# One lasting pool of weight tiles, and slabs in the space of an early part, in a one-core decoder layer

## The chip, the cores and the metric

The kernel runs on one core of a Trainium2 chip. Times are device microseconds (us). Three runs of the kernel before gave 1140.43, 1143.43 and 1144.64 us; the metric is the median, 1143.43 us.

## The reference

One decoder layer on x of 512 tokens by 2048 columns, in float32. h = RMSNorm(x); one combined projection of h (2048 columns to q, three pairs of k and v, gates, and four inputs of a second mixer); an attention mixer of 16 query heads in 4 groups with three branches (compressed, selected and window keys); a gated recurrence (HGRN2) of 8 heads; per-head RMSNorm and SiLU gates; one output projection, the residual, and a last RMSNorm. The piece that matters here is the compressed branch, which needs k and v in overlapping blocks of 32 tokens:

```python
def rmsnorm(x, g):
    xf = x.astype(jnp.float32)
    y = xf * lax.rsqrt(jnp.mean(xf * xf, axis=-1, keepdims=True) + EPS)
    return (y * g.astype(jnp.float32)).astype(x.dtype)

def compress_blocks(kv, pe, w1, w2):
    B, S, G, dh = kv.shape
    n_cmp = (S - CMP_BLOCK) // CMP_STRIDE + 1
    idx = CMP_STRIDE * np.arange(n_cmp)[:, None] + np.arange(CMP_BLOCK)[None, :]
    blk = kv[:, idx] + pe[:, None, :]
    blk = blk.transpose(0, 1, 3, 2, 4).reshape(B, n_cmp, G, CMP_BLOCK * dh)
    return jax.nn.gelu(blk @ w1) @ w2
...
    kc = compress_blocks(k_cmp, pe_k, w1_k, w2_k)
    vc = compress_blocks(v_cmp, pe_v, w1_v, w2_v)
    logits = jnp.einsum('btgrd,bngd->bgrtn', q, kc).astype(jnp.float32) - slopes * dist_c
...
    o = g[..., 0:1] * o_cmp + g[..., 1:2] * o_slc + g[..., 2:3] * o_win
```

## The kernel before

All large products are in float32 with each operand split in two parts of a shorter type: `hi` is a cast (ScalarE, L301) and `lo` the rest (VectorE, L302), and every product is three matmuls, hi x hi, hi x lo and lo x hi. A weight tile `w` is 128 partitions x 1024 float32, 4 KB a partition; a loaded tile takes one tile for the raw weights and two for its parts. Loads of weights are issued on SP's queue (`load_raw`, L160; in the seven-product part also L416). h^T lies in SBUF in 16 blocks of 128x512, each as hi and lo (`hh_`, `hl_`).

The program has two parts. In the first, k and v of the compressed branch (`first_proj`, `second_proj`) and two value projections are made, sums of blocks of h^T are formed (`all_sums`; the spaces `s2` and `s14`), and two wide projections are computed with seven block products in place of eight (`seven`, L405 to L505; products L453 to L455, plain ones L463 to L465; `in_turn` keeps two loads ahead). For these, `third_sums` saves block 21 of h^T to DRAM by POOL (L390) and puts a sum in its place; `block_21_back` brings it back, by POOL (L398). The results `y` are finished by `z_done` and stored to DRAM by POOL (L539). `first_part` holds the spaces of this part: `s2`, `s14`, twenty weight tiles `w`, and `e`.

When the first part is closed, a second pool of ten weight tiles (WBUF) and one of 25 slabs (`sl()`, 128x512 float32 each) take its space, so that their first tiles wait for the last use of what lay there. Then:

- `blocks(kf, 32)` loads k in two shifted copies by POOL (L607 to L610) into slabs, and VectorE adds the position terms (L621); `masks` and some clearing follow on POOL.
- `make_kd(0, 0)` and `make_q(0)` are projections (`proj_fm`: matmuls L555 to L557, 24 of them to a weight tile), run in turn with `compress` of k (weights L628, matmuls L637, a GELU, then L653). What they make is split and copied between partition halves on SP's queue (`split_dma`, L682 to L687); POOL casts the copies into the window's keys (L707, L708).
- `rows_back(vt_scr)` loads the value tokens `v_tok` into four slabs on SP's queue (L1072); `blocks(vf, 48)` does for v what was done for k.
- `make_kd(0, 1)`, `make_q(1)` and `make_kd(1, 0)` run in turn with `compress` of v. Attention, the recurrence, gates and the output projection follow, with the other projections as filling.

A scheduler sets the order on each engine from the program's priorities and its own times of the operations; each engine then works through its order. DMA issues wait in their queue's order, and a queue's DMAs go round on eight semaphores (`DMAHW0` to `DMAHW7` for SP, `DMASW0` to `DMASW7` for POOL).

Of the kernel before, what the change touches and what calls it, by code (L numbers as in the profile page):

```python
# [17 lines left out]
P = 128  # L18
# [11 lines left out]
WCOLS = 1024  # L30
WBUF = 10
NSLAB = 25
# [1 line left out]
PJ = 4  # L34
AHEAD = 2
FILL = (44, 42, 40, 24)
NU = 20
NE = 8
PAIRS = 6
AHEAD7 = 2  # L40
# [3 lines left out]
C_Q, C_KC, C_VC, C_KS, C_VS, C_KW, C_VW, C_GT, C_ZA = 0, 1024, 1280, 1536, 1792, 2048, 2304, 2560, 2608  # L44
C_QH, C_FH, C_IH, C_ZH = 3632, 4656, 5680, 6704
# [3 lines left out]
def hymba_layer(ctx: ExitStack, tc: tile.TileContext, x, norm_in, w_in, pe_k, w1_k, w2_k,  # L49
                pe_v, w1_v, w2_v, lower_bounds, nsa_norm, hgrn_norm, w_out, final_norm, out):  # L50
    nc = tc.nc
# [7 lines left out]
    small = ctx.enter_context(tc.tile_pool(name="small", bufs=2))  # L59
    psum = ctx.enter_context(tc.tile_pool(name="psum", bufs=1, space=bass.MemoryType.PSUM))  # L60

    cnt = [0, 0]

    def nm(s):
        cnt[0] += 1
        return f"{s}_{cnt[0]}"


    space, first_part = {}, ExitStack()
    wbufs = [NU]  # L70
    for name in ("s2", "s14", "w", "e"):
        space[name] = first_part.enter_context(tc.tile_pool(name=name + "_first", bufs=1))
    scr = ctx.enter_context(tc.tile_pool(name="scr", bufs=1, space=bass.MemoryType.DRAM))

    def sl(dt=FP32):
# [2 lines left out]
    def ev():  # L78
        return space["e"].tile([P, 512], FP32, name=nm("e"), tag="e", bufs=NE)

    def dram(shape=(P, 512)):
        n = nm("d")
        return scr.tile(list(shape), FP32, name=n, tag=n, bufs=1)
# [5 lines left out]
        return big.tile([P, 2048], dt, name=nm(tag), tag=tag, bufs=1)  # L89

    def b4(dt):
        return space["w"].tile([P, WCOLS], dt, name=nm("w"), tag="w", bufs=wbufs[0])

    def pj():
        return psum.tile([P, 512], FP32, name=nm("pj"), tag="pj", bufs=PJ)
# [13 lines left out]
    def run(*gens):  # L109

        st = [[g, t, 0.0] for g, t in gens]
        while st:
            e = min(st, key=lambda e: e[2] / e[1])
            try:
                c = next(e[0])
                e[2] = max([o[2] / o[1] for o in st if o is not e]) * e[1] + 1e-6 if c is None else e[2] + c
            except StopIteration:
                st.remove(e)

    def chain(*gens):  # L120
        for g in gens:
            yield from g
# [35 lines left out]
    def load_raw(src, k0, kt, c0, c):  # L158
        raw = b4(FP32)[:, 0:kt * c].rearrange("p (k c) -> p k c", k=kt)
        nc.sync.dma_start(out=raw, in_=src[k0 * P:(k0 + kt) * P, c0:c0 + c].rearrange("(k p) c -> p k c", p=P))  # L160
        return raw
# [4 lines left out]
    for k0, kt in FIRST:  # L166
        cs = slice(k0 * P, (k0 + kt) * P)
        first_w.append(load_raw(w_in2, k0, kt, C_KC, 256))
        if kt == 2:
            w = b4(FP32).rearrange("p (t c) -> p t c", t=4)  # L170
            for i in range(2):
                nc.sync.dma_start(out=w[:, 2 * i:2 * i + 2],
                                  in_=x2[i * 256:(i + 1) * 256, cs].rearrange("(t p) c -> p t c", p=P))
            xt.append([w[:, t] for t in range(NT)])
        else:
            w = [b4(FP32).rearrange("p (t c) -> p t c", t=2) for _ in range(2)]
# [177 lines left out]
    def corner(q, part):  # L354
        return hb[part][q][:, 0:4:2, 256:512]
# [30 lines left out]
    def third_sums():  # L386

        for q in range(PAIRS // 2):
            for part in range(2):
                nc.gpsimd.dma_start(out=a21[part][q], in_=corner(q, part).bitcast(FP32))  # L390
            hi, lo = [corner(q, part) for part in range(2)]
            nc.scalar.copy(hi, s3[q])
            nc.vector.tensor_tensor(lo, s3[q], hi.bitcast(FP32), ALU.subtract)

    def block_21_back():
        for q in range(PAIRS // 2):
            for part in range(2):
                nc.gpsimd.dma_start(out=corner(q, part).bitcast(FP32), in_=a21[part][q])  # L398
# [1 line left out]
    w_half = w_in2.rearrange("(j h p) c -> h p j c", h=2, p=P)  # L400
    free_banks = [(pj, pj), (pj, pj), (ps_lp, ps_lp), (ps_tp, ps_ot)]

    def seven(c0, done):


        t2, banks, acc, room = {}, {}, {}, {}
# [33 lines left out]
        def give(*names):  # L440
            for name in names:
                free_banks.append(banks[name])
# [24 lines left out]
        def after_first():  # L467
            room["u2"], room["u3"] = [ev(), ev()], [ev(), ev()]
            for tt in range(2):
                nc.scalar.copy(room["u2"][tt], acc["1"][tt])  # L470
            for tt in range(2):
                add(room["u2"][tt], acc["6"][tt], room["u2"][tt])
                add(room["u3"][tt], acc["7"][tt], room["u2"][tt])
            give("6", "7")

        def after_second():
            for tt in range(2):
                done(0, tt, acc["1"][tt], ev())
            for tt in range(2):
                y = ev()  # L480
                add(y, acc["4"][tt], room["u3"][tt])
                done(0, 2 + tt, y, y)
            give("4", "1")
# [34 lines left out]
    def in_turn(steps):  # L518
        ready = []
        for n in range(len(steps) + AHEAD7):  # L520
            if n < len(steps):
                ready.append(steps[n][0]())
            if n >= AHEAD7:
                steps[n - AHEAD7][1](ready[n - AHEAD7])
# [3 lines left out]
    vt_scr = [dram() for _ in range(NT)]  # L528
# [5 lines left out]
    def z_done(which):  # L534
        def done(half, t, src, y):
            th = ev()
            nc.scalar.activation(th, src, AF.Tanh, scale=rs[:, 1, t:t + 1])
            nc.vector.scalar_tensor_tensor(y, th, 1.0, src, ALU.add, ALU.mult)
            nc.gpsimd.dma_start(out=z_scr[which][half][t], in_=y)  # L539
        return done  # L540
# [49 lines left out]
    vc_bd, v_tok = [], []  # L590
# [10 lines left out]
    def blocks(acc, pcol):  # L601

        kv = []
        for j in range(2):
            f = acc[j]
            e, o = sl(), sl()
            nc.gpsimd.dma_start(out=e[0:64, :], in_=f[0:64, :])  # L607
            nc.gpsimd.dma_start(out=e[64:128, 0:511], in_=f[0:64, 1:512])
            nc.gpsimd.dma_start(out=o[0:64, :], in_=f[64:128, :])
            nc.gpsimd.dma_start(out=o[64:128, 0:511], in_=f[64:128, 1:512])  # L610
            kv += [e, o]
        blk = [sl() for _ in range(4)]
        for uq in range(4):
            b4_ = blk[uq].rearrange("p (u g n) -> p u g n", u=4, g=4)
            nc.gpsimd.memset(b4_[:, :, :, 31:32], 0.0)
            pe = col[:, pcol + uq * 4:pcol + uq * 4 + 4].unsqueeze(2).broadcast_to([P, 4, 31])
            for g in range(4):
                src = kv[g].rearrange("p (n u two) -> p u n two", u=8, two=2)
                n0 = uq // 2
                sv = src[:, (uq % 2) * 4:(uq % 2) * 4 + 4, n0:n0 + 31, 0]  # L620
                nc.vector.tensor_tensor(b4_[:, :, g, 0:31], sv, pe, ALU.add)  # L621
        return blk
# [70 lines left out]
    def make_kd(g2, b):  # L693


        acc = []
        yield from proj_fm(acc, (C_KS, C_KW)[b] + g2 * P, P)
        if b == 0:
            t = [sl(F32R) for _ in range(4)]
            v = t  # L700
        else:
            t = [space["att"].tile([P, 672], F32R, name=nm("kw"), tag="kw", bufs=KWB) for _ in range(4)]
            v = [a[:, 160:672] for a in t]
            for i in range(4):
                g = 2 * g2 + i // 2
                src = (kc_hi, kc_lo)[i % 2]
                nc.gpsimd.tensor_copy(t[i][:, 0:P], kd[g][0][i % 2][:, 0:P].bitcast(FP32))  # L707
                nc.gpsimd.tensor_copy(t[i][:, P:160], src[:, g * 32:(g + 1) * 32].bitcast(FP32))  # L708
        split_dma(acc[0], 1.0, [(v[0], 0, 0, 0), (v[0], 1, 0, 0), (v[1], 0, 1, 0), (v[1], 1, 1, 0),
                                (v[2], 0, 0, 1), (v[2], 1, 0, 1), (v[3], 0, 1, 1), (v[3], 1, 1, 1)])  # L710
        kd[2 * g2][b], kd[2 * g2 + 1][b] = t[0:2], t[2:4]

    def make_q(p):
        acc = []
        yield from proj_fm(acc, C_Q + p * P, P)
        qe, qo = sl(F32R), sl(F32R)
        split_dma(acc[0], -DH ** -0.5, [(qe, 0, 0, 0), (qe, 1, 1, 0), (qo, 0, 0, 1), (qo, 1, 1, 1)])
        q2[2 * p], q2[2 * p + 1] = qe, qo
# [347 lines left out]

    hq, hf_, hv = {}, {}, {}

    def rows_back(scr_, alloc):
        tiles = [alloc() for _ in range(NT)]  # L1070
        for t in range(NT):
            nc.sync.dma_start(out=tiles[t], in_=scr_[t])  # L1072
        return tiles

    def hgrn_qf(c):
# [73 lines left out]
    with tc.manual_schedule(engines={mybir.EngineType.PE, mybir.EngineType.Activation, mybir.EngineType.DVE}):  # L1149
# [4 lines left out]
    run((chain(second_proj(VC), proj_tm([], w_in2, hT, C_VS, 256, vs_done), proj_tm([], w_in2, hT, C_VW, 304, vw_done)),  # L1154
         70), (all_sums(), 7))
    third_sums()
    in_turn(seven(C_IH, v_done) + seven(C_ZA, z_done(0)))
    first_part.close()
    slabs = ctx.enter_context(ExitStack())
    wbufs[0] = WBUF  # L1160
    for name in ("w", "slab"):
        space[name] = slabs.enter_context(tc.tile_pool(name=name, bufs=1))
    att = ExitStack()
    space["att"] = att.enter_context(tc.tile_pool(name="att", bufs=1))
    block_21_back()
    kblk = blocks(kf, 32)
    masks()
    vc_bd += [sl() for _ in range(2)]
    for v in vc_bd:
        nc.gpsimd.memset(v, 0.0)  # L1170
    run((chain(make_kd(0, 0), make_q(0)), 22), (compress(kblk, w1_k, w2_k, True), 10))
    v_tok += rows_back(vt_scr, sl)
    vblk = blocks(vf, 48)
    run((chain(make_kd(0, 1), make_q(1), make_kd(1, 0)), 33), (compress(vblk, w1_v, w2_v, False), 33))
    fill = [make_q(2), make_q(3), make_kd(1, 1)] + [make_q(p) for p in range(4, 8)]
# [124 lines left out]
```

## Time and profile before

| | |
|---|---|
| median of three runs | 1143.43 us |
| the profiled execution's own time | 1139.92 us |
| its span, first to last instruction | 1138.2 us |
| mean granted clock of TensorE | 0.99 |
| PE busy / VectorE / ScalarE / POOL | 1094.7 / 656.7 / 419.2 / 97.3 us |
| moved by DMA | 127.44 MB |

The span is the time between the first and the last instruction that the profiler recorded; the execution's own time is 1.7 us longer. PE is TensorE's matmul work. PEclk is the share of TensorE's full clock (2.4 GHz) that was granted; the lower level, 1.2 GHz, is 0.5. A wait names the engine or DMA that released the waiting instruction last. Times in the rows count from the start of the span.

### The profile page before, as it was taken

What the parts mean: (1) busy time and instruction counts of PE and PEld (TensorE: products, weight loads), DVE (VectorE), ACT (ScalarE), POOL (GpSimd) and SP (SyncE); (2) the same over time, 40 slices, a digit from 0 to 9 for tenths busy, and PEclk for the clock granted to TensorE, in tenths of its full rate; (3) what the DMA queues carried; (4) which work ended last, traced back from release to release, by engine and by line L of the source; (5) the groups of instructions that cost most, each with busy time, mean ns of one, the idle gap of its engine ahead of it and who ended that gap; (6) DMA issues with size and microseconds to landing.
All of it is one profiled execution on the core that took longest, in us unless ns stands there. A gap on an engine that the chain in (4) does not pass through costs nothing.

```text
span 1138.2 us, 15228 instructions
## 1 busy us (share of the span) xinstructions
PE 1094.7 (96%) x5610; PEld 883.8 (78%) x5610; DVE 656.7 (58%) x1549; ACT 419.2 (37%) x835; POOL 97.3 (9%) x174
## 2 busy tenths in 40 slices
PE   7999999998859999999999999999999999999996
PEld 6899887876748777777777787888788788888886
DVE  4855756754424566675766466666567789424333
ACT  6534333332113564554555122222222343323211
POOL 1000000101611002020100000000000000102010
PEclk9999999999989999999999999999999999999998
DMA  9434345532885422232221323222121623335223
GB/s 312 150 104 138 127 146 191 165 127 81 202 223 130 112 57 56 56 75 56 58 72 39 111 58 109 74 75 74 57 74 56 232 84 105 101 117 173 97 84 120
DMA packets 100009, 127.44 MB, mean 112 GB/s; under 512 B 6672, under 2 KB 62176, under 8 KB 99936
## 3 DMA queue, kind: packets, MB, share of 16 engines
q1 hardware_dynamic: 94944, 114.95, 33.8%
q0 software_dynamic: 2688, 8.39, 2.3%
q10 hardware_dynamic: 2304, 3.15, 0.8%
q8 instruction: 44, 0.72, 0.3%
q14 instruction: 29, 0.24, 0.1%
HBM read 106.01 MB, written 12.06 MB: 104 GB/s over the span
## 4 chain that ended last, share of the span: by engine, by line
PE 90%; DMA 3%; DVE 3%; ACT 1%; issue 1%; POOL 1%; SPq 0%; ACTq 0%; POOLq 0%
PE pj L555 8%; PE pj L556 8%; PE pj L557 8%; PE pj L580 8%; PE pj L581 8%; PE pj L582 8%; PE ot L822 4%; PE pj L803 3%; PE lp L971 2%; PE pj L453 2%; PE pj L455 2%; PE pj L454 2%; DMA w<-in_w_in_dram 2%; PE lp L789 2%; PE lp L790 1%; PE pj L1232 1%
## 5 line engine op out<-in xcount | busy, mean ns | idle before, releaser
L302 DVE TENSOR_TENSOR w<-w,w 128x1024 fp32r<-128x1024 f32 (+3 forms) x169 | 202.6, 1211 | 163.4 <-ACT w L301 76.7
L301 ACT CAST w<-w 128x1024 fp32r<-128x1024 f32 (+3 forms) x169 | 172.1, 1036 | 250.4 <-DMA w<-in_w_in_dram 133.0
L555 PE MATMUL pj<-hh,w 128*128 128x512 f32 x448 | 187.0, 417 | 17.6 <-ACT w L301 17.0
L556 PE MATMUL pj<-hl,w 128*128 128x512 f32 x448 | 182.4, 407 | 0.0
L557 PE MATMUL pj<-hh,w 128*128 128x512 f32 x448 | 179.9, 402 | 0.1
L580 PE MATMUL pj<-w,hh 128*128 128x512 f32 (+2 forms) x352 | 127.9, 364 | 0.0
L581 PE MATMUL pj<-w,hl 128*128 128x512 f32 (+2 forms) x352 | 126.7, 361 | 0.0
L582 PE MATMUL pj<-w,hh 128*128 128x512 f32 (+2 forms) x352 | 126.7, 360 | 0.0
L555 PEld LDWEIGHTS pj<-hh,w 128*128 128x128 f32 x448 | 85.4, 191 | 39.1 <-ACT w L301 17.8
L557 PEld LDWEIGHTS pj<-hh,w 128*128 128x128 f32 x448 | 85.1, 190 | 20.6 <-DVE w L302 1.5
L556 PEld LDWEIGHTS pj<-hl,w 128*128 128x128 f32 x448 | 85.5, 191 | 17.5 <-issue 1.3
L758 DVE CUSTOM_DVE_ANT_0 s<-s,lp 128x128 f32<-128x128 f32 (+3 forms) x128 | 60.3, 482 | 46.9 <-PE lp L790 38.1
L763 ACT ACTIVATE s<-s,mn 128x128 f32<-128x128 f32 (+3 forms) x128 | 71.5, 560 | 33.7 <-DVE mn L758 18.6
L582 PEld LDWEIGHTS pj<-w,hh 128*128 128x128 f32 x352 | 66.3, 188 | 9.7
L580 PEld LDWEIGHTS pj<-w,hh 128*128 128x128 f32 x352 | 66.3, 189 | 9.3
L581 PEld LDWEIGHTS pj<-w,hl 128*128 128x128 f32 x352 | 66.3, 188 | 9.1
L803 PE MATMUL pj<-ident,s 128*128 128x128 f32 x320 | 54.0, 276 | 0.6 <-ACT s L763 0.3
L822 PE MATMUL ot<-pt,s 128*64 128x512 f32 (+3 forms) x256 | 49.0, 440 | 0.0
L803 PEld LDWEIGHTS pj<-ident,s 128*128 128x128 f32 x320 | 39.2, 140 | 10.8 <-ACT s L763 4.8
L812 ACT COPY pt<-pj 128x256 f32<-128x256 f32 (+2 forms) x56 | 25.6, 458 | 56.0 <-PE pj L803 55.7
L822 PEld LDWEIGHTS ot<-pt,s 128*64 128x64 f32 x256 | 23.0, 136 | 22.0 <-issue 11.0
L580 PE MATMUL pj<-w,s 128*128 128x512 f32 x96 | 37.7, 393 | 0.0
(345 smaller groups left out, 1914.6 us busy)
## 6 DMA issues: line engine op xcount, KB each, us to landing
w<-in_w_in_dram SPq DMA_DIRECT2D x121, 512.0 KB, 3.7
w<-in_w_out_dram SPq DMA_DIRECT2D x32, 512.0 KB, 3.6
s<-s SPq DMA_DIRECT2D x48, 128.0 KB, 2.3
w<-in_x_dram SPq DMA_DIRECT2D x16, 256.0 KB, 6.8
d<-e POOLq DMA_DIRECT2D x12, 256.0 KB, 3.2
s<-d SPq DMA_DIRECT2D x12, 256.0 KB, 5.8
l<-in_x_dram SPq DMA_DIRECT2D x12, 256.0 KB, 5.0
out_dram<-l SPq DMA_DIRECT2D x12, 256.0 KB, 2.8
```

The source lines that it names most:

```text
L301: nc.scalar.copy(hi, raw)
L302: nc.vector.tensor_tensor(lo, raw, hi.bitcast(FP32), ALU.subtract)
L555: nc.tensor.matmul(acc[j], wh, hh, start=kk == 0, stop=False)
L556: nc.tensor.matmul(acc[j], wh, hl, start=False, stop=False)
L557: nc.tensor.matmul(acc[j], wl, hh, start=False, stop=kk == NK - 1)
L580: nc.tensor.matmul(o, ah, hi[:, k, :], start=kk == 0, stop=False)
L581: nc.tensor.matmul(o, al, hi[:, k, :], start=False, stop=False)
L582: nc.tensor.matmul(o, ah, lo[:, k, :], start=False, stop=kk == NK - 1)
L758: nc.vector.tensor_tensor_reduce(out=y, in0=e["bias"][:, 384 - i * P:512], in1=lp, scale=1.0, scalar=3e38, op0=ALU.add, op1=ALU.min, accum ...
L763: nc.scalar.activation(y, y, AF.Exp, bias=mn, scale=-1.0, accum_out=e["ls"][:, 2 * i + b:2 * i + b + 1])
L803: nc.tensor.transpose(tps[:, j * P:(j + 1) * P], y[:, j * P:(j + 1) * P], ident)
L822: nc.tensor.matmul(e["ot"][b * 64:(b + 1) * 64, j * P:512], v_tok[j][:, b * 256 + g * DH:b * 256 + (g + 1) * DH], e["pt"][:, b, j * 512:38 ...
```

## The change

- NU falls from 20 to 10. A pool `w` of ten weight tiles (WBUF) is opened at the start and lasts to the end of the kernel; a pool `more_w` of ten lives in the first part. `b4` takes tiles from the two by turns while `more_w` is there, and from `w` alone afterwards.
- When the first part closes, only the slabs take its space (`s2`, `s14`, `more_w`, `e`); no weight pool is opened there.
- `rows_back` takes the issuing engine as an argument, and `v_tok` is loaded on POOL's queue; the other calls stay on SP's.
- `block_21_back` is no longer called behind `first_part.close()` but inside the second `seven`, in `after_first`, once the group with the third sum is done.

```diff
-NU = 20
+NU = 10
...
-    wbufs = [NU]
-    for name in ("s2", "s14", "w", "e"):
-        space[name] = first_part.enter_context(tc.tile_pool(name=name + "_first", bufs=1))
+    space["w"] = ctx.enter_context(tc.tile_pool(name="w", bufs=WBUF))
+    for name in ("s2", "s14", "more_w", "e"):
+        space[name] = first_part.enter_context(tc.tile_pool(name=name, bufs=1))
...
     def b4(dt):
-        return space["w"].tile([P, WCOLS], dt, name=nm("w"), tag="w", bufs=wbufs[0])
+        cnt[2] += 1
+        if "more_w" in space and cnt[2] % 2:
+            return space["more_w"].tile([P, WCOLS], dt, name=nm("w"), tag="w", bufs=NU)
+        return space["w"].tile([P, WCOLS], dt, name=nm("w"), tag="w", bufs=WBUF)
...
-    def seven(c0, done):
+    def seven(c0, done, then=lambda: None):
...
             give("6", "7")
+            then()
...
-    def rows_back(scr_, alloc):
+    def rows_back(scr_, alloc, eng=nc.sync):
         tiles = [alloc() for _ in range(NT)]
         for t in range(NT):
-            nc.sync.dma_start(out=tiles[t], in_=scr_[t])
+            eng.dma_start(out=tiles[t], in_=scr_[t])
...
-    in_turn(seven(C_IH, v_done) + seven(C_ZA, z_done(0)))
+    in_turn(seven(C_IH, v_done) + seven(C_ZA, z_done(0), block_21_back))
     first_part.close()
-    slabs = ctx.enter_context(ExitStack())
-    wbufs[0] = WBUF
-    for name in ("w", "slab"):
-        space[name] = slabs.enter_context(tc.tile_pool(name=name, bufs=1))
+    del space["more_w"]
+    space["slab"] = ctx.enter_context(tc.tile_pool(name="slab", bufs=NSLAB))
...
-    block_21_back()
...
-    v_tok += rows_back(vt_scr, sl)
+    v_tok += rows_back(vt_scr, sl, nc.gpsimd)
```

How the instructions move. The lines of the changed kernel lie three or four further on (L160 is L163 there, L628 is L632, L687 is L691, L607 is L611).

First place, SP's queue at the end of the sevens, with the semaphores waited for: `w_2243` is the last weight of the sevens, `w_2440` and `w_2495` are the two tiles of `make_kd(0, 0)`, `w_2458`, `w_2485` and `w_2513` weights of compress k, `w_2554` the first tile of `make_q(0)`. Before:

```order
L160 DMA w_2243<-in_w_in_dram 128x2x512 [waits DMAHW2_49,DVE_49]
L160 DMA w_2440<-in_w_in_dram 128x8x128 [waits DMAHW4_49,DMAHW3_49,DMAHW5_49,DMAHW1_49,DMAHW6_49,DMAHW0_49,DMAHW7_49,DVE_49,PE_49]
L628 DMA w_2458<-in_cmp_w_k_dram 128x4x256
L628 DMA w_2485<-in_cmp_w_k_dram 128x4x256
L160 DMA w_2495<-in_w_in_dram 128x8x128
L628 DMA w_2513<-in_cmp_w_k_dram 128x4x256
L160 DMA w_2554<-in_w_in_dram 128x8x128
```

and in the changed program, where the last weight of the sevens is `w_2252`:

```order
L163 DMA w_2252<-in_w_in_dram 128x2x512 [waits PE_49]
L163 DMA w_2440<-in_w_in_dram 128x8x128 [waits PE_49]
L632 DMA w_2458<-in_cmp_w_k_dram 128x4x256 [waits DMAHW1_49,DMAHW0_49,PE_49]
L632 DMA w_2485<-in_cmp_w_k_dram 128x4x256 [waits DMAHW7_49,DVE_49]
L163 DMA w_2495<-in_w_in_dram 128x8x128 [waits DMAHW2_49,PE_49]
L632 DMA w_2513<-in_cmp_w_k_dram 128x4x256 [waits DMAHW2_49,DVE_49]
L163 DMA w_2554<-in_w_in_dram 128x8x128 [waits DMAHW4_49,PE_49]
```

`w_2440` no longer waits for the eight queues, VectorE and PE, but for one count of PE, which the matmul 120 before the last one of the sevens reaches; the issues behind it wait for a semaphore or two each. Six of these weight tiles, `w_2440` to `w_2554`, wait for matmuls that lie before the end of the sevens.

Second place, SP's queue between the weights of compress v (`w_2758` is the last of the four) and the weight `w_2768`, the second tile of `make_kd(0, 1)`; `s_2637` and `s_2638` are the halves of q's first rows, `s_2649` to `s_2652` are `v_tok`. Before:

```order
L628 DMA w_2758<-in_cmp_w_v_dram 128x4x256
L687 DMA s_2637<-s_2640 64x512
L687 DMA s_2637<-s_2641 64x512
L687 DMA s_2638<-s_2640 64x512
L687 DMA s_2638<-s_2641 64x512
L1072 DMA s_2649<-d_178 128x512
L1072 DMA s_2650<-d_179 128x512
L1072 DMA s_2651<-d_180 128x512
L1072 DMA s_2652<-d_181 128x512
L160 DMA w_2768<-in_w_in_dram 128x8x128
```

and in the changed program:

```order
L632 DMA w_2758<-in_cmp_w_v_dram 128x4x256
L163 DMA w_2768<-in_w_in_dram 128x8x128
L691 DMA s_2637<-s_2640 64x512
L691 DMA s_2637<-s_2641 64x512
L691 DMA s_2638<-s_2640 64x512
L691 DMA s_2638<-s_2641 64x512
L163 DMA w_2854<-in_w_in_dram 128x8x128
```

The weight stands ahead of q's four copies instead of behind them, and the four loads of `v_tok` are gone from this queue.

Third place, POOL between the last casts of the window's keys (`kw_`) and the v blocks (`s_2657` to `s_2664`). Before:

```order
L708 CAST kw_2828<-kc_lo 128x32
L708 CAST kw_2830<-kc_lo 128x32
L607 DMA s_2657<-d_672 64x512
L608 DMA s_2657<-d_672 64x511
L609 DMA s_2658<-d_672 64x512
L610 DMA s_2658<-d_672 64x511
```

and in the changed program:

```order
L712 CAST kw_2828<-kc_lo 128x32
L712 CAST kw_2830<-kc_lo 128x32
L1076 DMA s_2649<-d_181 128x512
L1076 DMA s_2650<-d_182 128x512
L1076 DMA s_2651<-d_183 128x512
L1076 DMA s_2652<-d_184 128x512
L611 DMA s_2657<-d_675 64x512
L612 DMA s_2657<-d_675 64x511
L613 DMA s_2658<-d_675 64x512
L614 DMA s_2658<-d_675 64x511
```

The four `v_tok` loads stand ahead of the v blocks. The six copies of block 21, which the text of the program calls earlier now, stand at the same place in POOL's order in both.

On PE the matmuls are the same 4567 rows; behind the sevens the changed order runs the 48 matmuls of `make_kd(0, 0)` and one of `make_q(0)` before compress k (before: 21 of `make_kd(0, 0)`), and 162 projection matmuls in all before compress v (before: 128).

## Rows read from the trace of the kernel before

**Rows 1.** Page, part 1 (busy us, share, instructions) and part 6 (KB each, us to landing).
```profile
PE 1094.7 (96%) x5610; PEld 883.8 (78%) x5610; DVE 656.7 (58%) x1549; ACT 419.2 (37%) x835; POOL 97.3 (9%) x174
...
d<-e POOLq DMA_DIRECT2D x12, 256.0 KB, 3.2
```

**Rows 2.** Waits of PE, 60 to 277 us: line, releaser, us in total, times, longest.
```profile
PE pj L453 <- ACT w L301: 1.4, 1, 1.4
```

**Rows 3.** Waits of PE, 277 to 340 us.
```profile
PE pj L555 <- ACT w L301: 17.0, 2, 11.6
PE lp L637 <- issue: 3.0, 1, 3.0
```

**Rows 4.** Waits of PE, 340 to 1138 us, the largest.
```profile
PE lp L971 <- ACT s L1000: 1.1, 3, 0.8
```

**Rows 5.** Timeline of PE, 276 to 341 us: start, us, line, operation [idle before <-releaser].
```profile
276.10 0.40 PE L465 MATMUL pj<-w,hh 128*128 128x512 f32 x1
281.84 0.79 PE L555 MATMUL pj<-hh,w 128*128 128x512 f32 x1 [5.35 <-ACT w L301]
...
288.36 0.40 PE L557 MATMUL pj<-hh,w 128*128 128x512 f32 x1
...
289.77 0.39 PE L557 MATMUL pj<-hh,w 128*128 128x512 f32 x1
293.15 2.02 PE L637 MATMUL lp<-s,w 128*128 128x128 f32 x16 [2.99 <-issue]
...
315.31 0.61 PE L653 MATMUL tp<-s,s 128*128 128x128 f32 x4
...
335.70 0.79 PE L555 MATMUL pj<-hh,w 128*128 128x512 f32 x1 [11.62 <-ACT w L301]
...
340.01 7.38 PE L637 MATMUL lp<-s,w 128*128 128x128 f32 x64 [0.23 <-issue]
```

**Rows 6.** Windows: us, busy us (count) of PE, PEld, DVE, ACT, POOL; PEclk, DMA share, GB/s.
```profile
220.00:260.00 40.00, 38.62 (x166) 30.80 (x165) 23.77 (x25) 15.16 (x17) 2.67 (x5) 1.00 0.41 132
260.00:280.00 20.00, 16.50 (x72) 13.05 (x70) 9.82 (x13) 4.25 (x6) 3.17 (x6) 1.00 0.16 43
280.00:290.00 10.00, 8.12 (x21) 5.76 (x21) 3.09 (x7) 1.04 (x1) 7.15 (x22) 0.66 1.05 311
290.00:300.00 10.00, 7.01 (x47) 6.28 (x47) 6.45 (x14) 2.09 (x2) 10.00 (x15) 1.00 0.94 242
320.00:330.00 10.00, 4.08 (x18) 2.96 (x16) 1.31 (x3) 0.00 (x0) 1.35 (x7) 0.96 1.06 237
335.00:340.00 5.00, 4.04 (x8) 2.35 (x9) 4.32 (x13) 1.69 (x2) 0.00 (x0) 0.55 0.40 112
```

**Rows 7.** Timeline of SP's queue, 276 to 325 us.
```profile
276.53 0.37 SPq L160 DMA_DIRECT2D w<-in_w_in_dram  x1
...
322.47 1.99 SPq L1072 DMA_DIRECT2D s<-d  x4
```

**Rows 8.** The chain that ended last, 278 to 335 us: start, us, what.
```profile
278.12 7.10 DMA d<-e
...
318.52 0.70 DVE s L682
...
319.89 8.11 DMA s<-s
328.07 6.51 DMA w<-in_w_in_dram
```

**Rows 9.** DMA view, 270 to 340 us: bytes, and issues (KB, median us to landing).
```profile
DMA packets 15988, 14.40 MB, mean 206 GB/s; under 512 B 1648, under 2 KB 14064, under 8 KB 15984
...
s<-d SPq DMA_DIRECT2D x4, 256.0 KB, 8.5
```

**Rows 10.** Timeline of POOL, 316 to 319 us.
```profile
316.93 0.55 POOL L607 DMA_DIRECT2D s<-d  x1
...
318.50 0.52 POOL L610 DMA_DIRECT2D s<-d  x1
```

More of the change, by code (lines that the diff above doesn't have):

```diff
@@ L60, in hymba_layer @@
     psum = ctx.enter_context(tc.tile_pool(name="psum", bufs=1, space=bass.MemoryType.PSUM))
-    cnt = [0, 0]
+    cnt = [0, 0, 0]
     def nm(s):
```

## The prediction

> **What bounds the kernel now.** I read the page first, then the waits of PE (TensorE) stretch by stretch, then PE's timeline where the waits lie, then the queues that feed it. The page [rows 1] says that PE is the bound: busy 1094.7 us of a span of 1138.2. All that isn't PE's own work is 43.5 us, so a change that adds and removes no matmul can win only there, and in time that PE spends at a low clock.
>
> The waits by stretch tell where that is. Between 60 and 277 us, where the seven-product projections ("the sevens") run, the largest is 1.4 us [rows 2]; after 340 it is 1.1 [rows 4]. The 63 us between hold 17.0 us of waiting for the cast of a weight tile, in two waits, and 3.0 at the compress matmuls [rows 3]. The timeline of PE [rows 5] gives their places: 5.35 us before 281.84 (first matmul of `make_kd(0, 0)`), 2.99 before 293.15 (first matmul of compress k), 11.62 before 335.70 (second half of `make_kd(0, 1)`). Together 19.96 us.
>
> Behind the first and the third wait PE is also slow. From 288.36 to 289.77 six matmuls take 1.41 us, 0.235 each. Fourteen start between 281.84 and 288.36: 6.52 us where 14 x 0.235 = 3.29 would do, 3.2 lost. Eight start between 335.70 and 340.01: 4.31 less 8 x 0.235 = 1.88 and 0.23 of idle, 2.2 lost. The granted clock agrees [rows 6]: 0.66 in 280-290 and 0.55 in 335-340, toward the lower level (1.2 GHz is 0.5), after PE had been idle for 5 and 12 us; behind the 2.99 us it stayed 1.00. So the two long waits cost 5.4 us more.
>
> Why the weights are late: the first weight after the sevens is issued on SP at 276.53 [rows 7], when the last matmul of the sevens has just begun (276.10 in [rows 5]). Until then the DMA engines were busy 41% and 16% of their time (220-260, 260-280); from there on 1.05, 0.94 and 1.06, at 237 to 311 GB/s [rows 6]. The third wait is a chain [rows 8]: the small copies of q's split tiles take 8.11 us, until 328.07; only then does SP issue the weight, which takes 6.51.
>
> **The change part by part.** *Weight pool.* Before, the ten tiles of the later part lie in the first part's space, so the first of them waits for all that used it: in the order eight semaphores of DMA queues, VectorE and PE. Now ten tiles live through the kernel, and that row waits for one matmul that lies 120 before the end of the sevens: 120 x 0.235 = 28 us earlier; after a landing of 6.51 it is some 21 us ahead of need. Six of the tiles now go out before 276.5, into engines that were not half busy. The wait of 5.35 goes, and the 3.2 behind it. What was late in the third wait, `w_2768`, is issued ahead of q's copies in the new order and no longer behind them: 11.62 and 2.2 go.
>
> In the first part itself twenty tiles become ten and ten, taken by turns, so that a tile still reuses the one twenty before it: nothing added. The wait of 1.4 was for a cast behind late weights, and weights stand further ahead of their use now; I let it go (ends 0 and 1.4).
>
> *Slabs in the space of the sums.* They still wait for the end of the first part, so the k blocks start no earlier: the store of k lands 7.10 us after 278.12, at 285.22 [rows 8], and the last block load and the additions bring compress to 293.15 [rows 5], 7.9 later. In the new order 49 matmuls stand between the sevens and compress k, up to 276.5 + 49 x 0.235 = 288.0. Upper end: the chain stays as it is, 5.1 of idle. Lower end: with six weights out of its way the store lands in the whole run's 3.2 [rows 1], and 1.2 is left, or nothing. I take 2.5, near the middle, since the four tiles of compress k still share the engines. Of the 2.99 this gives back 0.5.
>
> *v_tok on POOL.* SP loses four issues, 1.99 us together [rows 7]; POOL gets four at 0.52 [rows 10], 2.1 us, ahead of the v blocks. Who waits: compress v. POOL comes to them behind the casts of kc. Before the kc matmuls stand 84 of `make_kd` and `make_q` (19.7) and compress k (64 matmuls took 7.38 in the compress at 340.01 [rows 5]): 276.5 + 19.7 + 7.4 + 2.5 = 306.1. In before these start at 315.31 and POOL's first v block at 316.93 [rows 5, 10], 1.6 later; so 307.7, v_tok to 309.8, eight v blocks to 314.0, and 7.9 as above: 321.9. Compress v comes after 162 matmuls and compress k, 276.5 + 38.1 + 7.4 + 2.5 = 324.5. Not late by this sum; ends 0 and 3, I take 1.
>
> Does the other queue bring anything of itself? With the engines at 1.06 [rows 6] the 1 MB takes what it takes; only SP's 1.99 us are freed. The Trainium skill, page "DMA: Bandwidth & Descriptors", section "Issuing engines are not separate DMA queues", says so and more: transfers of all issuers end on the same 16 engines, and a second issuer saves only the time of issuing. By that rule this edit wins nothing and only the early start does; carried to the whole stage it is rival one.
>
> *Block 21 back earlier.* In the order of POOL these six copies stand at the same place with the same neighbours in both programs: nothing.
>
> *w_2768.* It is needed after 118 matmuls and compress k, 276.5 + 27.7 + 7.4 = 311.6. On SP the four tiles of compress v stand ahead of it. Ends: 0 (issued before 305, landing 6.51) and 9 (rival one); I take 1, as most of what is ahead of it was issued early.
>
> Sum: 19.96 + 5.4 + 1.4 = 26.8 out, 2.5 + 1 + 1 = 4.5 in, net 22.3. After 340 the longest wait is 1.1 [rows 4] and PE's order there is nearly the same, so nothing takes it back. Against the profiled run: 1139.9 - 22.3 = 1117.6. That run lies 3.5 us (0.3%) under the median of the three; against the median 1143.4 - 22.3 = **1121**. Less than 0.5% (5.7 us) counts as no change here.
>
> **The rivals.** *One: the engines hold the stage, not the issue.* 14.40 MB move between 270 and 340 [rows 9]. The six early tiles (512 KB each) are 3.1 MB; the other 11.3 at 260 GB/s, about the middle of the saturated windows [rows 6], need 43 us: until 320. If what PE needs at 311 comes last, it waits 9 us and loses 2.2 to the clock, besides the 2.5 at compress k: 26.8 - 13.7 = 13 won, 1130. For: the saturated windows. Against: v_tok and the tiles of `make_kd(1, 0)` are last in line, and nobody needs them at 311. Chance 0.20.
>
> *Two: no new wait at all.* The engines are free early enough for the k blocks too: 26.8 won, 1116.6. For: the store's 3.2 at other times; against: the blocks' chain still begins behind the sevens. Chance 0.13.
>
> *Three: the change doesn't do what it says.* The early tiles are held by something that the order doesn't price, and the stage starts as it does now: 1143. Against: the one matmul waited for lies 28 us ahead. Chance 0.07.
>
> *Four, slower: v_tok holds POOL.* Each of its loads waits, in the new order, for earlier loads of POOL's queue. If they ran one behind another, at the 8.5 us that they take from SP [rows 9], they would hold POOL for 34 us, from 307.7 to 342; eight v blocks (4.2) and 7.9 put compress v at 354 in place of 324.5: 29.5 of idle and 3 of clock, with 3.5 of the other waits 36 in against 26.8 out, 9 slower: 1152. It decides when compress v starts later than about 350. Against: POOL's loads issue back to back, four within 1.57 us of each other [rows 10]. The Trainium skill, page "SBUF — State Buffer", section "SBUF: two separate sides", warns that a load issued from GpSimd starves while VectorE runs in a mode that takes both ports; no run here shows such a case, and the POOL issue at 318.50 [rows 10], beside VectorE's work at 318.52 [rows 8], took 0.52 like the others. Chance 0.05.
>
> **How the numbers follow.** My own case has the rest, 0.55, with 1117 to 1126 by its ends. The range of 1112 to 1135 takes in case two with some 4 us of spread between runs below it, and case one with as much above; it leaves out cases three and four and a tail, under 0.2. Faster by over 0.5% (below 1137.7): my case, one and two, 0.88, less 0.02 for a case one twice as bad, 0.86. Same: three and that tail, 0.09. Slower: 0.05.
>
> **What would show it.** Right: the first weight of `make_kd` issued near 248 us; PE's first matmul behind the sevens without idle; a granted clock of 1.00 throughout 280-340; one wait of 1 to 5 us before compress k; `make_kd(0, 1)` without the 11.6; and from the end of compress v on the same time as before. Wrong: a weight wait of over 5 us near 311 with saturated engines (rival one); POOL idle between v_tok's loads (rival four); the sevens ending later than 276.5; waits that grow after 340.

## The result and the profile after

The changed kernel takes 1125.01 us (median of four runs, 1124.3 to 1125.52); the kernel before, timed beside it, 1142.68 (1140.43 to 1144.64). The ratio is 0.9846, with a 95% interval of 0.9825 to 0.9866: 17.7 us less. The prediction was 22.3 less, 1121 us, with a range of 1112 to 1135. The direction and the range held; the gain was a fifth smaller than forecast. (Three kernels below that differ from this one only in the small edits gained 14.8 to 15.8 us over the kernel before, each timed beside it.) The two profiled executions, 1139.92 and 1124.61 us, are 15.3 apart, and it is between these that the time is followed here.

PE's waits between 277 and 340 us, which answer to [rows 3] (line, releaser, us in total, times, longest); the lines lie four further on than before. Where a row below names `issue`, the profile shows nothing that the engine waited for. Between 60 and 277 us the list is empty (before: [rows 2]):

```profile
PE lp L641 <- POOL s L286: 4.9, 1, 4.9
PE pj L559 <- ACT w L304: 3.2, 1, 3.2
PE pj L561 <- DVE w L305: 0.4, 1, 0.4
```

8.5 us in place of 19.96. Their places in the timeline of PE (start, us, line, operation, [idle before <-releaser]), against [rows 5]:

```profile
275.01 0.40 PE L468 MATMUL pj<-w,hh 128*128 128x512 f32 x1
275.25 0.39 PE L559 MATMUL pj<-hh,w 128*128 128x512 f32 x1
...
286.44 0.40 PE L559 MATMUL pj<-hh,w 128*128 128x512 f32 x1
291.78 8.22 PE L641 MATMUL lp<-s,w 128*128 128x128 f32 x48 [4.95 <-POOL s L286]
299.76 0.48 PE L560 MATMUL pj<-hl,w 128*128 128x512 f32 x1
...
324.02 0.40 PE L561 MATMUL pj<-hh,w 128*128 128x512 f32 x1
327.59 0.50 PE L559 MATMUL pj<-hh,w 128*128 128x512 f32 x1 [3.17 <-ACT w L304]
...
331.51 0.39 PE L561 MATMUL pj<-hh,w 128*128 128x512 f32 x1
...
333.84 7.30 PE L641 MATMUL lp<-s,w 128*128 128x128 f32 x64
```

The first matmul of `make_kd(0, 0)` follows the last of the sevens after 0.24 us, like any other: the wait of 5.35 and the slow matmuls behind it are gone. `make_kd(0, 1)` runs through: the 11.62 are gone too. Two long waits are left. Compress k (291.78) comes 4.95 us after PE ran out of work, and `make_q(1)` (327.59) 3.17 us. Both have a slow stretch behind them. From 291.78 to 299.76 the 48 compress matmuls take 7.98 us; the 64 from 333.84 take 7.06 to the next start (340.90), so 48 would take 5.3: 2.7 lost. From 327.59 to 331.51 eight projection matmuls take 3.92 us, where 1.88 and the 0.37 of idle would do: 1.7 lost. Idle and slow together, 8.5 + 4.4 = 12.9 us; before, 25.4.

The releaser that the profile names for compress k, a mask on POOL (L286), writes a slab that compress k doesn't read. What it does read are the sums of k and the position terms, and VectorE began the last twelve of these at 288.54, after a wait for loads of the k blocks:

```profile
288.54 3.97 DVE L625 TENSOR_TENSOR s<-s,col 128x124 f32<-128x124 f32 x12 [2.54 <-DMA s<-d]
```

The windows (us, busy us of PE, PEld, DVE, ACT, POOL with counts, PEclk, DMA share, GB/s), against [rows 6]:

```profile
220.00:260.00 40.00, 40.00 (x174) 32.44 (x173) 22.21 (x23) 13.87 (x15) 3.41 (x6) 1.00 0.54 170
260.00:280.00 20.00, 20.00 (x88) 16.18 (x87) 8.91 (x12) 5.00 (x6) 3.81 (x7) 1.00 0.34 100
280.00:290.00 10.00, 6.84 (x30) 5.17 (x28) 3.02 (x9) 1.04 (x1) 9.37 (x23) 1.00 1.05 277
290.00:300.00 10.00, 8.22 (x49) 8.25 (x50) 6.62 (x13) 1.56 (x2) 8.99 (x16) 0.66 0.11 22
300.00:310.00 10.00, 10.00 (x54) 8.39 (x53) 1.65 (x4) 0.91 (x3) 1.18 (x4) 1.00 1.04 289
...
320.00:325.00 5.00, 4.42 (x19) 3.20 (x18) 0.00 (x0) 0.00 (x0) 0.00 (x0) 1.00 1.12 230
325.00:330.00 5.00, 2.04 (x5) 1.26 (x6) 2.43 (x6) 2.09 (x2) 0.00 (x0) 0.80 1.00 229
```

The granted clock falls to 0.66 in 290-300 and 0.80 in 325-330, toward the lower level, each time behind an idle PE. The DMA share tells the rest. Before the end of the sevens the engines now do more (0.54 and 0.34, before 0.41 and 0.16). Then they are full in 280-290, **nearly empty in 290-300 (0.11, 22 GB/s)**, and full from 300 to 330. SP's queue shows why (start, us, line, what):

```profile
247.87 0.37 SPq L163 DMA_DIRECT2D w<-in_w_in_dram  x1
...
263.97 0.37 SPq L163 DMA_DIRECT2D w<-in_w_in_dram  x1
...
280.80 6.20 SPq L163 DMA_DIRECT2D w<-in_w_in_dram  x2
...
298.25 0.37 SPq L632 DMA_DIRECT2D w<-in_cmp_w_v_dram  x1
...
306.97 0.37 SPq L163 DMA_DIRECT2D w<-in_w_in_dram  x1
314.62 2.48 SPq L691 DMA_DIRECT2D s<-s  x4
317.19 2.02 SPq L163 DMA_DIRECT2D w<-in_w_in_dram  x2
```

The first weight of `make_kd` goes out at 247.87, where 248 was forecast, and the sixth at 263.97. The next weights leave up to 287.0 (the row of 280.80 is two issues, the second behind a wait for its tile). Then nothing leaves for 9.9 us: the first weight of compress v, at 298.25, waits for compress k's matmuls (L641), which have to use up its tile first, and PE was waiting for compress k. From there on everything comes at once. q1's first weight stands behind q's copies, for which SP waits 7.2 us, until ScalarE has split q. Waits of SP, 280 to 330 us:

```profile
SPq L632 <- PE lp L641: 10.4, 2, 9.9
SPq L691 <- ACT s L687: 7.2, 1, 7.2
```

So that weight is issued at 317.19, and its cast begins 9.3 us later (ScalarE's timeline):

```profile
326.49 1.04 ACT L304 CAST w<-w 128x1024 fp32r<-128x1024 f32 x1 [10.94 <-DMA w<-in_w_in_dram]
```

The balance of the two profiled runs. The last matmul of the sevens begins at 275.01 and not at 276.10, 1.1 us earlier. Waits and low clock behind them fall by 25.4 - 12.9 = 12.5. The first scores of attention (L775, now L779) begin at 361.0 and not 375.2, 14.2 earlier, of which this explains 13.6. The last matmul of the recurrence's L971 (L975) begins 15.1 earlier (862.1, before 877.2), and the span is 15.3 shorter: about one us more comes in small pieces, and nothing is given back.

### The profile page after: what moved, and what is told of

It is laid out like the page before. It is cut to its first block, busy times and chain, and to the rows that moved or that the text cites. A ratio compares the mean times of both kernels' runs of the same rounds, so it can differ in the third digit from the quotient of the medians.

```text
span 1122.9 us, 15245 instructions
## 1 busy us (share of the span) xinstructions
PE 1093.9 (97%) x5610; PEld 885.7 (79%) x5610; DVE 658.5 (59%) x1549; ACT 420.1 (37%) x835; POOL 99.9 (9%) x178
## 5 line engine op out<-in xcount | busy, mean ns | idle before, releaser
L305 DVE TENSOR_TENSOR w<-w,w 128x1024 fp32r<-128x1024 f32 (+3 forms) x169 | 204.8, 1217 | 173.9 <-ACT w L304 79.1
L304 ACT CAST w<-w 128x1024 fp32r<-128x1024 f32 (+3 forms) x169 | 172.9, 1036 | 283.6 <-DMA w<-in_w_in_dram 148.3
L826 PE MATMUL ot<-pt,s 128*64 128x256 f32 (+3 forms) x256 | 48.3, 440 | 0.0
L826 PEld LDWEIGHTS ot<-pt,s 128*64 128x64 f32 x256 | 22.5, 136 | 21.9 <-issue 11.6
```

The costliest lines, as they stand in the source:

```text
L304: nc.scalar.copy(hi, raw)
L305: nc.vector.tensor_tensor(lo, raw, hi.bitcast(FP32), ALU.subtract)
L826: nc.tensor.matmul(e["ot"][b * 64:(b + 1) * 64, j * P:512], v_tok[j][:, b * 256 + g * DH:b * 256 + (g + 1) * DH], e["pt"][:, b, j * 512:38 ...
```

## Which of the edits did it

**The old pools with the two small edits.**

```diff
# before.py
-    def rows_back(scr_, alloc):
+    def rows_back(scr_, alloc, eng=nc.sync):
...
-    block_21_back()
...
-    v_tok += rows_back(vt_scr, sl)
+    v_tok += rows_back(vt_scr, sl, nc.gpsimd)
```

> Before, with the two small edits alone (v_tok on POOL's queue, block 21 called back inside the sevens); the pools are those of before. Theory, the pools carry the gain: about as before, 1139 to 1146 us, with the wait of some 5 us behind the sevens and a second long one. Rival, the move of v_tok off SP's queue carries a good part of it (the weight behind it then goes out some 2 us earlier and q's copies no longer hold it): 1130 to 1137.

Measured: 1139.34 us, ratio 0.9991 (0.9975 to 1.0007), no change. Waits of PE, 276 to 345 us:

```profile
PE pj L556 <- ACT w L301: 15.5, 2, 9.9
PE lp L638 <- POOL s L283: 3.6, 1, 3.6
```

Taking v_tok off SP lets the weight of `make_kd(0, 1)` out at 324.14 instead of 328.07, and the wait before it is 9.9 and not 11.6; PE's work is put in another order, and the end does not come earlier.

**The pools alone.** The changed kernel with `rows_back(vt_scr, sl)` on SP and `block_21_back()` behind the first part.

> The changed kernel with the two small edits undone: only the pools differ from before. Theory: the gain stays, 1125 to 1130, no wait behind the sevens, the wait before compress k near 5 us, and the wait for q1's first weight (3.2 us in the changed kernel) some 2 us longer as v_tok's four issues stand ahead of it on SP. Rival, the small edits are needed for it: 1131 to 1140.

Measured: 1124.05 us, 0.9853 (0.9833 to 0.9873): the whole gain. Waits of PE:

```profile
PE lp L641 <- DMA w<-in_w_in_dram: 4.2, 1, 4.2
PE pj L559 <- ACT w L304: 2.3, 1, 2.3
PE pj L561 <- DVE w L305: 0.5, 1, 0.5
```

The pools carry it. Their edit also gave the scheduler another order (`w_2768` ahead of q's copies, for one); the lasting tiles and that order were not tried apart. The wait before compress k was as expected; the one for q1's weight did not grow by v_tok's issues.

**v_tok back on SP, alone.**

```diff
-    v_tok += rows_back(vt_scr, sl, nc.gpsimd)
+    v_tok += rows_back(vt_scr, sl)
```

> The changed kernel with v_tok back on SP's queue. Theory, SP's order decides when q1's first weight goes out: it is issued 2 us later and the wait of 3.2 us grows to 5 or more, with a low clock behind it: 1127 to 1130. Rival, the DMA engines decide, not the queue: no difference, 1124 to 1126.

Measured: 1124.48 us, 0.9851 (0.9826 to 0.9876): no difference from the changed kernel, as the rival had it. The chain at that place (start, us, what):

```profile
318.17 6.41 DMA w<-in_w_in_dram
```

q1's weight goes out one us later than in the changed kernel (318.17, there 317.19) and lands in 6.41 us, so that its cast begins at 324.66 and not at 326.49. With v_tok on POOL the v blocks stand behind it and go out from 313.81 on, where here they go out from 308.93, so that more of them is on the engines together with the weight. What the queue won, the slower landing took back. The Trainium skill, page "DMA: Bandwidth & Descriptors", section "Issuing engines are not separate DMA queues", states that the transfers of all issuers share the same 16 engines, and that a second issuer saves only the time of issuing; these two runs agree (1 us of issue, and 1124.48 against 1125.01 us).

**Block 21 back late, alone.** `block_21_back()` behind `first_part.close()`.

> The changed kernel with block 21 called back behind the first part, as before. As predicted, POOL's order has these copies at the same place: nothing, 1124 to 1126. Rival: with lasting weight tiles make_kd no longer waits for the first part, so the copies' place in the program matters now, and PE waits for block 21 behind the sevens: 1127 to 1132.

Measured: 1125.06 us, 0.9864 (0.9843 to 0.9884). Nothing, as predicted: the interval overlaps that of the changed kernel. PE's first wait behind the sevens is again the one before compress k (4.4).

## What the two waits that are left come from

**Compress k begun later.**

```diff
-    run((chain(make_kd(0, 0), make_q(0)), 22), (compress(kblk, w1_k, w2_k, True), 10))
+    first_q = chain(make_kd(0, 0), make_q(0))
+    for _ in upto(first_q, 16.0):
+        pass
+    run((first_q, 22), (compress(kblk, w1_k, w2_k, True), 10))
```

> The changed kernel with compress k begun after make_kd(0, 0) and nearly all of make_q(0): 96 projection matmuls behind the sevens and not 49, so 11 us more of cover for the k blocks. Theory: the wait of 4.9 us before compress k and the low clock behind it (2.7 us) go: 1116 to 1119. Rival, the transfers of the stage only shift and the wait turns up before compress v or q1: 1122 to 1126.

Measured: 1126.71 us, 0.9879 (0.9859 to 0.9898), not better than the changed kernel. Waits of PE, the chain at that place, and the DMA view of 300 to 323 us:

```profile
PE pj L559 <- ACT w L304: 11.8, 1, 11.8
```

```profile
305.00 16.44 DMA w<-in_w_in_dram
```

```profile
DMA packets 5639, 5.88 MB, mean 256 GB/s; under 512 B 774, under 2 KB 4934, under 8 KB 5638
```

The wait before compress k is gone, with its low clock (1.00 in 280 to 310), and a wait of 11.8 us stands before a tile of `make_kd(0, 1)`. Its weight was issued at 305.00, in good time, and took 16.44 us, beside 5.88 MB that moved at 256 GB/s. This is the mechanism of rival one of the prediction, in another order.

**Eleven lasting tiles.**

```diff
-WBUF = 10
+WBUF = 11
-NSLAB = 25
+NSLAB = 23
-NU = 10
+NU = 9
```

> The changed kernel with 11 lasting weight tiles, 9 for the early part and 23 slabs: in its order q1's first weight stands ahead of the copies of q's first rows on SP. Theory, that weight is late because its tile comes free late and the copies hold it: it goes out near 308 and not 317 us, and the wait of 3.2 us with its low clock (1.7) goes: 1119 to 1122. Rival, the saturated engines (300 to 330 us) bring it no earlier: 1124 to 1126.

Measured: 1120.49 us, 0.9822 (0.9797 to 0.9846), an interval that still overlaps that of the changed kernel. Waits of PE and the window in which the engines had been empty:

```profile
PE lp L641 <- issue: 3.4, 1, 3.4
PE lp L641 <- POOL s L286: 2.2, 1, 2.2
```

```profile
290.00:300.00 10.00, 10.00 (x67) 9.50 (x67) 2.20 (x3) 0.62 (x1) 7.74 (x15) 0.85 0.67 166
```

q1's wait is gone, as the theory had it; in this kernel's order its weight stands ahead of q's copies and was out by 309.5. The first weight of compress v goes out at 292.07 and not 298.25, and the engines are 0.67 busy in 290-300 and not 0.11. Compress k began 2.9 us earlier here (288.87), which accounts for that much of the 6.2; the rest agrees with the reading of SP's rows, that the ten tiles made the gap. The edit changed the tiles, the slabs and the order together, so that the tile alone isn't shown to have done it. The wait before compress k is shorter (2.2), which the edit had not been meant to do. A wait of 3.4 us before compress v, until 329.96, is new. PE's releaser isn't shown; VectorE's sums for compress v began at 326.30, behind the second part (L305, 325.15) of a weight that had come late.

**v_tok late.** `v_tok += rows_back(...)` behind the run with compress v.

> The changed kernel with v_tok loaded behind the v blocks and after make_kd(1, 0) in the program, out of the way of both. Theory, in the changed kernel v_tok's 1 MB on POOL makes q1's first weight land in 9.2 us where the kernel with v_tok on SP had 6.5: here it lands in 6.5 or less from an issue near 317, and the wait of 3.2 us falls to under 1: 1120 to 1123. Rival, other loads (compress v, v blocks) make it late: 1124 to 1126.

Measured: 1127.16 us (1123.63 to 1128.92), 0.9876 (0.985 to 0.9902). Waits of PE in the profiled execution, which is the fastest of the four:

```profile
PE lp L641 <- POOL s L286: 5.7, 1, 5.7
PE lp L641 <- issue: 1.2, 1, 1.2
PE pj L561 <- DVE w L305: 0.4, 1, 0.4
```

The mechanism came as expected: q1's weight, issued at 315.72, is cast at 321.48, and only 0.4 us of its wait is left. The time did not follow. In the profiled execution the stage up to the first scores of attention takes 82.5 us and not 86.0 from the last matmul of the sevens, in spite of a longer wait before compress k (5.7), but from the first to the last scores it takes 232.1 and not 228.6: what the stage won is lost again there. The other three runs are 2.7 to 5.3 us slower than the profiled one; what differs in them stays open.

**The z stores on SP's queue.** `nc.sync.dma_start` for L543.

> The changed kernel with the z stores on SP's queue, so that POOL's loads of the k blocks are not issued in turn with them: the last of eight goes out near 280 and not 282.8 us. Theory, the queue in which the loads stand decides: the wait of 4.9 us before compress k falls to 2 or 3: 1121 to 1123. Rival, the engines decide (1.05 busy at 280 to 290, the k loads land in 6 to 8 us): 1124 to 1126, or worse if the stores hold SP's weights.

Measured: 1127.84 us, 0.9884 (0.9865 to 0.9904). Waits of PE:

```profile
PE lp L641 <- issue: 5.0, 1, 5.0
PE pj L559 <- ACT w L304: 4.8, 1, 4.8
```

All eight k loads are issued by 278.85 (changed kernel: 283.3) and compress k begins at 288.49 and not 291.78, so the place of the loads in POOL's queue does count. But the order made for this kernel runs 39 matmuls ahead of compress k and not 49, and PE waits the same 5.0 us for it; the wait for q1's weight has grown to 4.8. Neither theory as it stood.

## Spreading the transfers

**The v blocks and v_tok early.**

```diff
     kblk = blocks(kf, 32)
+    vblk = blocks(vf, 48)
     masks()
+    v_tok += rows_back(vt_scr, sl, nc.gpsimd)
...
-    v_tok += rows_back(vt_scr, sl, nc.gpsimd)
-    vblk = blocks(vf, 48)
```

> The changed kernel with the v blocks and v_tok loaded right behind the k blocks, ahead of and behind the masks on POOL, where the engines of the changed kernel stand nearly idle (0.11 busy, 22 GB/s in 290 to 300 us). Theory, what is left of the waits is the engines being crowded from 300 to 330 us: q1's first weight lands in some 6 and not 9.2 us and its wait (3.2, 0.4 and 1.7 of low clock) goes: 1118 to 1122. Rival, the ten tiles hold the weights, not the engines: the wait stays at 3 us or turns up at compress v: 1124 to 1127.

Measured: 1121.16 us, 0.9835 (0.9806 to 0.9864); in the theory's range, but the interval overlaps that of the changed kernel (0.9825 to 0.9866), so the time alone doesn't decide it. Waits of PE and a window:

```profile
PE lp L641 <- POOL s L619: 4.5, 1, 4.5
PE lp L641 <- issue: 2.3, 1, 2.3
PE tp L657 <- DVE s L652: 1.0, 1, 1.0
```

```profile
290.00:300.00 10.00, 9.85 (x58) 9.48 (x59) 8.26 (x21) 1.05 (x1) 10.00 (x16) 0.77 0.57 137
```

With v's 2 MB partly in the empty stretch (0.57 busy, in the changed kernel 0.11) no cast of a weight is left among PE's waits. A late weight still counts, by another way. ScalarE's timeline:

```profile
314.66 1.04 ACT L304 CAST w<-w 128x1024 fp32r<-128x1024 f32 x1 [13.15 <-DMA w<-in_w_in_dram]
315.61 0.43 ACT L647 COPY s<-lp 128x128 f32<-128x128 f32 x2
```

The copy of compress k's sums out of the two PSUM buffers `lp` stands behind the cast of a weight that waited for its load, and compress v, whose sums go to the same two buffers, begins 0.36 us after the copy (315.97), at the end of its wait of 2.3.

**Early v and compress later together.**

> The edits of the compress-later run and of the early-v run together. In the first, the weight of make_kd(0, 1) issued at 305.00 landed after 16.4 us beside 5.88 MB of other loads, and PE waited 11.8. Theory, engines: without v's 2 MB beside it that wait is 0 to 4, and as the wait before compress k is gone too: 1112 to 1118. Rival, ten tiles: eight hold compress weights, the projection's weight goes out no earlier and the wait stays over 6: 1121 to 1127.

Measured: 1123.14 us (1119.32 to 1124.0), 0.9842 (0.9812 to 0.9873). The weight of `make_kd(0, 1)` is waited for 2.1 us and not 11.8: that part of the theory held. But 4.6 us turn up before compress k's second product, which waits for a GELU step on VectorE. The sum is no better than with early v alone.

**Early v, eleven tiles, compress k after 72 matmuls.**

> Early v, eleven lasting tiles (nine in the early part, 23 slabs), and compress k begun after 72 projection matmuls: each of the three takes one cause of the waits away. Theory: no wait over 2 us between 276 and 345 us, 1110 to 1116. Rival, PE's waits move behind the stage (attention, fewer slabs): 1117 to 1124.

Measured: **1118.6 us** (1117.2 to 1119.9), 0.9806 (0.9774 to 0.9838), the lowest median of these kernels: 21.4 us under the kernel before timed beside it, where the changed kernel was 17.7 under its own. The two intervals overlap. It lies in the rival's range, not in the theory's 1110 to 1116. One long wait is left, 7.0 us before compress k's second product. Timelines of VectorE (L650) and ScalarE (start, us, line, operation, [idle before <-releaser]):

```profile
313.39 0.53 DVE L650 TENSOR_TENSOR s<-s 128x256 f32<-128x256 f32 x1
319.48 1.04 ACT L304 CAST w<-w 128x1024 fp32r<-128x1024 f32 x1 [7.18 <-DMA w<-in_w_in_dram]
320.43 0.41 ACT L651 ACTIVATE s<-s 128x256 f32<-128x256 f32 x1
```

The tanh of the GELU (L651, 320.43) had its input at 313.92, when L650 ended, but it stands on ScalarE behind the cast of a weight (L304, 319.48), which waited 7.18 us for its load. Each engine works through its order, so a late weight holds work that doesn't need it.

How much better than the changed kernel these kernels are can be read inside the traces, one execution each, over the same matmuls. From the last matmul of the sevens to the last scores of attention it takes 328.1 us before, 314.6 in the changed kernel, 312.9 to 315.1 in the three kernels that differ from it by the small edits, 311.5 with eleven tiles, 311.5 with early v, and 312.8 here. So either of the two wins some 1 to 4 us, and having both, with compress k later, isn't shown to win more.

**The small compress weights early.** The last run adds to that one that the second weights of both compressions are loaded ahead of the k blocks.

> The run with early v and eleven tiles, in which PE waited 7.0 us before compress k's second product, because its 128 KB of weights stood on SP behind the eight copies of make_kd(0, 0) (309.15 us): here these two small loads are called before the k blocks. Theory, that order alone made the wait: no wait over 2 us in 276 to 345, 7 us and the low clock behind it (1.2 on that stretch) less, 1110 to 1113. Rival, the engines (1.10 busy at 300 to 320 us) hold the next weight instead: 1116 to 1120.

Measured: 1119.93 us (1118.7 to 1121.61, five runs), 0.981 (0.9785 to 0.9835): no gain. The theory fell: the wait moved and did not go. In this run PE waits 6.3 us before compress v, until 317.93, and ScalarE shows:

```profile
317.56 0.43 ACT L651 COPY s<-lp 128x128 f32<-128x128 f32 x2 [3.49 <-DMA s<-s]
```

The copy of compress k's sums (L651) into a slab is released at 317.56 by one of the copies on SP's queue, 3.49 us after ScalarE was free, and compress v needs the buffers that it empties. With 23 slabs and v's loaded early, a free slab is a likely reason; that was not tried by itself.

## Why the prediction was right, and where it was off

The range held, but it had been drawn wide enough to take in rival one (1130) too, so that alone says little for the sum. The gain of the two profiled executions, 15.3 us, lies nearer to that rival's 13 than to the 22.3 of the sum.

- *Where the time is*: right. All of the gain up to attention but 1.7 us lies between the last matmul of the sevens and compress v.
- *Weight pool*: right in mechanism and place, and in the size of what goes out (the lasting tiles together with the order that came with them). The first weight went out at 247.87 (forecast 248), the waits of 5.35 and 11.62 and the 5.4 us of low clock behind them went, and so did the 1.4 in the sevens. The pools alone give the whole gain.
- *Block 21*: nothing, as forecast. *v_tok on POOL*: that the other queue brings nothing of itself held; the 1 us that the sum took for a late compress v was 0, as no wait stands before its first matmul (333.84). Each edit was undone alone. v_tok's move even shows both sides, an issue 1 us earlier and a landing 3 us later.
- *The step that failed is the size of what is put in: 4.5 us forecast, 12.9 measured.* For compress k, 2.5 was taken between 1.2 (or nothing) and 5.1; the idle was 4.95, and 2.7 of low clock followed it. The chain behind this term had been misread. The row `278.12 7.10 DMA d<-e` is not the store of k, which L598 had sent to DRAM, with v, between 45 and 64 us; it is a store of z (L539), and two of POOL's loads of k waited for stores of z (1.7 and 0.4 us). That part came out near the lower end: the last k load was issued at 282.76 and not 285.51. But the 7.9 us that were carried over for the rest did not hold. Compress k began 9.0 us after the last load's issue (before: 7.6), as VectorE got its data only at 288.54, with the engines full in 280-290, and PE was ready at 286.8 and not at 288.0. The run with the z stores on SP bears on it: all k loads out by 278.85, compress k at 288.49. And the term had no clock in it, because the wait of 2.99 us before had left the clock at 1.00; behind 4.95 it fell to 0.66. The bound of 5.1 was itself too low by that. The sign of a clock at 1.00 throughout 280-340 failed with it.
- *`w_2768`*: taken at 1, measured 0; it was issued at 306.97 and there was no wait at its use. The wait came one tile later, at q1's first weight, 3.5 us and 1.7 of clock, which the sum had no term for. The mechanism is in part that of rival one (crowded engines), at another place and with half the price; the other part is SP's order, in which this weight stood behind q's copies. The result, 1125, lies between the forecast and that rival's 1130.
- *Rival one's rate* held: 289, 267, 230 and 229 GB/s in the four stretches from 300 to 330, 256 in the crowded stretch of the run with compress k later, 260 assumed. What it missed is that the engines would also stand empty, for ten us, in the middle of it.
- *Rivals two, three and four*: none. There were 8.5 us of new waits, and the early weights did go out early. POOL issued the four v_tok loads in 2.19 us, without a wait between them.

## What to carry to other kernels

A pool that begins in the space of a finished stage turns the end of that stage into the start of its loads; a few tiles that live through both keep the loads going, and here the pools alone were worth 1.5%. Once the first load is early, look at the transfers of the stage as a whole: a stretch of empty DMA engines ahead of a crowded one asks what the next load waits for, here a buffer. One more buffer, or a transfer moved into the gap, took some 1 to 4 us off in the traces here, another issuing queue nothing. A late weight can also hold up work that doesn't need it, when its cast stands ahead of that work on an engine. When a wait is taken away, price the next one with the low clock that its length may bring.

## What was not expected of the hardware

- How much clock a short wait costs could not be read off its length. In before, 2.99 us of idle left the granted clock at 1.00, and so did 2.31 in the run with early v (310-320); in the run with eleven tiles, 2.17 were followed by 0.85 in 290-300. Behind 4.95 us in the changed kernel it was 0.66, with 2.7 us of loss, and behind 3.17 us it was 0.80, with 1.7.
- Loads of 512 KB, all issued on SP, took 6.41 us (v_tok on SP), about 9.2 (changed kernel) and 16.44 (compress k later) from issue to landing in this stretch of full engines; the median of the whole changed run was 3.7.
